# Two short logit blocks in one visit, each merge round in one step, W of two pairs in one, and a new order of the steps

## The chip, the cores and the metric

The kernel runs on one core of one Trainium2 chip. The metric is the device time of one execution in microseconds (us). A core has a tensor engine (PE) with its weight loader (PEld), a vector engine (DVE), a scalar engine (ACT), a general engine (POOL) and a queue engine (SP) that issues transfers (DMAs). The engines run side by side and wait for each other by semaphores.

## The reference, cut to what matters

One decoder layer on 512 tokens of width 1024, all in float32: a norm, one input projection, two groups of eight heads side by side (block-sparse attention with a relative bias, and a gated delta rule in chunks of 64), one output projection, and an MLP of width 4096.

```python
h = rms_norm(x, pre_mix_norm)
att_q, att_k, att_v, gdn_qkv, gdn_z, gdn_a, gdn_b = split(h @ w_in)
# attention: at 512 tokens and blocks of 256 every past block is chosen, so it is causal
logits = q @ k.T * scale + rel_bias[bucket(distance)]
o_att  = softmax(causal(logits)) @ v
# gated delta rule, chunks of 64 tokens
a_mat = eye(64) + strict(k_beta @ k.T * decay)          # unit lower triangular
u, w  = solve(a_mat, v * beta), solve(a_mat, k_beta * exp(g_cum))
def step(state, chunk):                                  # 8 chunks, one after the other
    v_new = u - w @ state
    o     = q_dec @ state + (q @ k.T * decay) @ v_new
    state = state * exp(g_last) + k_dec.T @ v_new
x = x + rms_norm(concat(o_att, norm(o) * silu(z)) @ w_out, post_mix_norm)
h = rms_norm(x, pre_mlp_norm)
x = x + rms_norm(square(relu(h @ w_up)) @ w_down, post_mlp_norm)
```

## The kernel before

The first half of the layer (0 to about 300 us) is woven from generators. `Weave` holds a list of names, `STEPS`; it takes the first name in the list whose generator is ready, and runs that generator to its next `yield`. What PE does is issued in exactly that order. DVE, ACT and POOL are ordered by a scheduler, in which `LEAD` raises the priority of a kind of step; SP is ordered by hand from the loads of the output weights on. The MLP behind it (about 300 to 609 us) is ordered by hand on all engines.

The generators, and the names that they leave in the rows:

- `projections` (rows `ps_mm<-hT_h,w_hi`, `hT_l,w_hi`, `hT_h,w_lo`): the input projection. Weights and activations are split into a high and a low part, so each of the eight steps of an output block is three matmuls. `ORDER` lists the blocks: q, k, v of the delta rule, its gate z, and x, y for the attention; `w0` is V of the attention, made by token (`w_hi,hT_h`) in four banks, one of them in `ps_mm`. One step of `projections` is three matmuls, and they fill the room between all other work. The weights are cast on ACT (L137) and their low part is made on DVE or POOL (L138); `LO_DVE` says which.
- `chunks`: the matrices of a pair of heads for the delta rule (`RC,picks`; `ident,sqt` are transposes of the squares of q; `LWQ,kraw` is k and q against k inside a chunk).
- `scores`: attention logits of a pair of heads, one visit for each block q of 128 queries, with 128(q+1) keys, in the order q = 3, 2, 1, 0 (rows `ps_a<-pt`, six matmuls of 64 rows each); then for each head and block a minimum on DVE (L672) and an exponential on ACT (L674).
- `values`: for each block of keys, transposes of the exponentials (`ident,L`), a copy from the bank by ACT (`ph`, L700), and at last the transposed sums (`ident,R`), and the product with V (`ph,V`), which takes a bank `ps_a`.
- `inverse`: 31 rounds on DVE that invert the 32 x 32 diagonal blocks of `a_mat`. `scan` then merges them to 64 x 64: round 1 (`uap,NT`, 32 x 32 tiles), a copy by ACT, and round 2 (`inv,uap`). It makes W (`inv,kB`, 64 x 64 tiles) and runs the eight chunks (`S,LWQ`, `vn,kdec`, `vn,AT`, `vB,inv`). `z` is one of two halves of the heads; each half is four heads, two pairs.
- `finish_o` norms the output of the scan (`ot`, transposes `ident,ot`, product with the gate `om`, its high part `mg_h`).
- `weights_out` loads the output weights (`wo_raw`, L124), of which two buffers are there for the first eight; ACT casts them (`wo_h`, L125) and DVE makes the low part (L126). `output` is the output projection (`wo_h,mg_h`).
- `normed` norms x of a block of tokens, stores it (`d_x`, L996) and transposes it; `weights_up` and `up0` load the first up-projection's weights (the last ones by L132, `w_raw`) and run it (`mg_h,w_hi`).

Pieces of one kind that follow each other on PE are called a visit. The functions that the diff touches are these:

Of the kernel before, what the change touches and what calls it, by code (L numbers as in the profile page):

```python
# [11 lines left out]
FT = mybir.dt.float32  # L12
# [7 lines left out]
STEPS = "constants_in0 chunks1 constants_in0 bias0*3 chunks0 chunks2 chunks3 scalars0*2 ev0 ev1 ev_q0*2 ev_k0*2 inverse0 scores0 projections0 values0 projections0 scalars0 projections0 scalars0 projections0*5 bias0 projections0 ev2 projections0*4 scores0 ev0 projections0*2 ev1 projections0*2 ev3 scores0 values0 scalars0 chunks2 projections0*2 ev2 chunks0 scores0 chunks1 projections0*2 ev3 projections0 chunks3 chunks0 projections0 scores0 chunks0 projections0 scores0 ev4 chunks1 projections0 ev1 chunks1 projections0 ev3 projections0*4 ev4 projections0 chunks0 chunks1 projections0 chunks0 ev5 projections0 chunks0 projections0*5 chunks1 ev4 projections0 chunks1*2 projections0 ev5 ev6 projections0*8 ev7*2 projections0 chunks2*2 ev6 chunks2 projections0 chunks2 projections0*4 chunks3 projections0 chunks2 projections0 ev8 chunks3*2 projections0*4 chunks3 chunks2*2 projections0*3 ev8 projections0 ev_q1*2 projections0 chunks3 ev8 chunks3 projections0*5 chunks3 inverse0*5 projections0*12 inverse0 projections0*6 inverse0 projections0*2 inverse0 projections0*6 inverse0 projections0*5 inverse0 projections0 inverse0 projections0*2 values0 ev9 projections0*4 inverse0 values0 projections0 inverse0 projections0 inverse0*2 values0 chunks3 projections0 values0 projections0 inverse0*2 ev10 projections0 values0 projections0 inverse0 projections0 values0 projections0*4 inverse0 projections0 ev11 projections0*3 ev9*2 inverse0 projections0*2 ev10*2 inverse0 projections0 inverse0 projections0*7 inverse0 projections0 ev11 inverse0 projections0 inverse0 ev11 inverse0 projections0 ev_k1*2 projections0 ev12 scores0 projections0*3 ev12 projections0 inverse0 ev12 inverse0 projections0*2 inverse0 projections0*2 ev_q2*2 scores0 projections0 inverse0 projections0*2 inverse0*2 weights_out0 weights_up0 scan0 scores0 values0*2 projections0 scores0 projections0*2 values0 scores0 projections0*2 ev_k2*2 projections0 up00 output0 scores0 values0 scan0 scores0 values0*2 scan0 values0 scores0 scan0*3 scores0 projections0 scan0 values0*2 scores0 projections0 scan0 projections0 scores0 values0 scan0 scores0 values0 projections0 scan0*5 projections0*5 scan0 ev_q3*2 projections0*2 scan0 projections0*2 scan0 projections0*2 scan0 finish_o0 projections0 values0 scan0 values0*2 projections0 scan0 projections0 ev_k3 scores0 projections0 ev_k3 scan0 projections0 scan0 scores0 scan0 finish_o0 projections0 finish_o0 finish_o1 projections0*3 ev13 scores0 values0 ev13 values0 scan0 finish_o1*2 projections0*3 scan0 scores0 scan0 projections0 values0 scores0 finish_o2 projections0 scan0 projections0*3 ev14 scan0 ev14 values0 scores0 finish_o0*2 finish_o1 projections0 finish_o2 finish_o1 projections0 finish_o2*3 projections0 scan0 projections0*3 scan0 finish_o3 weights_out0 projections0*2 ev15 finish_o3 ev15 projections0 values0 weights_out0 values0 finish_o3*3 finish_o0 weights_out0*2 finish_o1 weights_out0*9 values0 finish_o2 weights_up0 weights_out0 output0 weights_out0*2 output0 later0 output0*2 weights_out0*2 later0 finish_o3 weights_up0 output0*10 weights_up0 output0*5 later0*2 output0 weights_up0 output0*5 weights_up0 output0 weights_up0 output0*4 weights_up0 output0*2 weights_up0 output0*6 normed0 normed1 output0*6 weights_up0 output0*9 normed2 output0 normed0 output0 weights_up0 output0 normed1 weights_up0 output0*10 up00 output0*2 normed3 up00 normed2 up00*2 normed3 up00*3"  # L20

LEAD = {'chunks': 100, 'inverse': 50, 'scan': 100, 'scores': 100, 'values': 300, 'finish_o': 200, 'take': 50, 'take_a': 100, 'scalars': 50}
# [5 lines left out]
ORDER = "k0 q0 x0 y0 k1 q2 q1 k2 k3 z0 q3 x1 w0 v1 v3 v2 v0 y1 x2 y2 x3 y3 z2 z1 z3"  # L28
LO_DVE = (22, 53)
# [42 lines left out]
def layer(ctx, tc, nc, x, x_t, x_t0, w_first, w_in, w_v, w_ab, w_out, w_up, w_down, conv_w, a_log, dt_bias, gdn_norm_w, rel_bias,  # L72
# [8 lines left out]
    def mm(o, l, r, **kw):  # L81
        nc.tensor.matmul(o, l, r, **kw)  # L82
# [564 lines left out]
    def scores():  # L647
        for p in range(4):
# [12 lines left out]
            for q in (3, 2, 1, 0):  # L661
                w = 128 * q + 128
                qs = slice(128 * q, 128 * q + 128)
                s = [bank("a") for _ in range(2)]
                for n, (i, j) in enumerate(((0, 2), (0, 3), (1, 2))):
                    for hh in range(2):
                        hs = slice(64 * hh, 64 * hh + 64)
                        mm(s[hh][:, :w], T[i][hs, qs], T[j][hs, :w], start=n == 0, stop=n == 2)
                for hh in range(2):
                    l = Ls[hh][:, 64 * q * (q + 1):64 * q * (q + 1) + w]  # L670
                    rows_of[p, hh, q] = l
                    nc.vector.tensor_tensor_reduce(out=l, in0=s[hh][:, :w], in1=Es[hh][:, w - 1::-1], scale=1.0, scalar=3e38,  # L672
                                                   op0=OP.add, op1=OP.min, accum_out=mins[:, q, hh:hh + 1])
                    act(l, l, AF.Exp, bias=mins[:, q, hh:hh + 1], scale=-1.0, accum_out=sums[:, q, hh:hh + 1])  # L674
                yield
                mark(f"row{p}{q}")
# [76 lines left out]
    def scan():  # L753
# [11 lines left out]

        for z in range(2):
            if z:
                yield
            p1 = bank(shape=(128, 4, 4, 32))
            for h in range(4):  # L770
                for t in range(4):
                    for c in range(2):
                        a, b = slice(64 * c, 64 * c + 32), slice(64 * c + 32, 64 * c + 64)
                        mm(p1[b, h, t], NT[a, 4 * z + h, t, 32:64], uap[z][a, h, t], start=True, stop=True,
                           tile_position=(64 * c, 64 * c + 32))
            for c in range(2):
                b = slice(64 * c + 32, 64 * c + 64)
                nc.scalar.copy(uap[z][b], p1[b])
        mark("p1")
        yield  # L780
        for z in range(2):
            if z:
                yield
            p2 = bank(shape=(128, 4, 4, 32))
            for h in range(4):
# [743 lines left out]
```

## Time and profile before

| | |
|---|---|
| time of one execution, median of 3 runs | 616.49 us (615.99 to 616.88) |
| profiled execution: its own time | 617.12 us |
| profiled execution: span of its profile | 615.3 us, mean granted clock 0.997 |
| last input projection ends | 235.4 us |
| output projection starts | 243.1 us |
| merge and scan | 167 to 232 us |
| transfers | 113.21 MB, mean 184 GB/s |

The rows are read so: start or group, length in us, engine, line of the kernel, operation, output<-inputs, and for a matmul rows x columns of the tile in the array, the shape of the moving operand and a count. In brackets stands how long the engine was idle before it, and who released it. "Busy" of PE includes a slow start; the start of the next row tells what a row cost.

### The profile page before, as it was taken

What the parts mean: (1) busy time and instruction counts of PE and PEld (TensorE: products, weight loads), DVE (VectorE), ACT (ScalarE), POOL (GpSimd) and SP (SyncE); (2) the same over time, 40 slices, a digit from 0 to 9 for tenths busy, and PEclk for the clock granted to TensorE, in tenths of its full rate; (3) what the DMA queues carried; (4) which work ended last, traced back from release to release, by engine and by line L of the source; (5) the groups of instructions that cost most, each with busy time, mean ns of one, the idle gap of its engine ahead of it and who ended that gap; (6) DMA issues with size and microseconds to landing.
All of it is one profiled execution on the core that took longest, in us unless ns stands there. A gap on an engine that the chain in (4) does not pass through costs nothing.

```text
span 615.3 us, 11043 instructions
## 1 busy us (share of the span) xinstructions
PE 604.2 (98%) x4281; PEld 516.7 (84%) x4281; DVE 475.5 (77%) x685; ACT 369.0 (60%) x645; POOL 138.0 (22%) x179
## 2 busy tenths in 40 slices
PE   9999999999999998999999999999999999999995
PEld 7777777878778786888999999999998888888884
DVE  6679973899735767757799878787788888887785
ACT  7379773354686686534358565755575557565663
POOL 1556845101231211025022231222121310000000
PEclk9999999999999999999999999999999999999998
DMA  8332324222722124813769998999999999768403
GB/s 310 92 112 85 89 87 100 96 79 85 176 76 79 36 65 138 312 70 136 291 170 317 252 249 233 280 268 211 277 313 327 299 296 285 244 218 301 165 0 137
DMA packets 61156, 113.21 MB, mean 184 GB/s; under 512 B 15784, under 2 KB 35368, under 8 KB 60720
## 3 DMA queue, kind: packets, MB, share of 16 engines
q1 hardware_dynamic: 43120, 82.89, 39.4%
q0 software_dynamic: 17696, 29.36, 22.8%
q8 instruction: 33, 0.54, 0.3%
q10 hardware_dynamic: 288, 0.26, 0.1%
q14 instruction: 19, 0.16, 0.1%
HBM read 106.71 MB, written 35.15 MB: 231 GB/s over the span
## 4 chain that ended last, share of the span: by engine, by line
PE 78%; issue 9%; DMA 5%; DVE 4%; ACT 1%; POOL 1%; SPq 0%; POOLq 0%; ACTq 0%; DVEq 0%
PE ps_mm L82 40%; PE ps_g L82 20%; PE ps_a L82 16%; DMA wo_raw<-in_w_out 2%; PE ps_a L85 2%; DMA xy<-d_x 1%; PE ps_g L85 1%; DMA w_raw<-in_w_up 1%; DVE wo_l L126 1%; POOL rkq L175 1%; DVE xs L995 0%; DMA ww<-in_w_first 0%; DMA w_raw<-in_w_in 0%; DVE conv L365 0%; ACT wo_h L125 0%
## 5 line engine op out<-in xcount | busy, mean ns | idle before, releaser
L113 ACT CAST wdh<-wd 128x1024 fp32r<-128x1024 f32 x53 | 55.9, 1054 | 51.4 <-PE ps_mm L82 22.6
L113 ACT CAST u_h<-w 128x1024 fp32r<-128x1024 f32 x49 | 51.0, 1045 | 51.2 <-DVE w L1139 15.6
L114 DVE TENSOR_TENSOR wdl<-wd,wdh 128x1024 fp32r<-128x1024 f32 x53 | 64.9, 1224 | 21.5 <-ACT wdh L113 21.4
L114 DVE TENSOR_TENSOR u_l<-w,u_h 128x1024 fp32r<-128x1024 f32 x49 | 59.9, 1224 | 23.4 <-ACT u_h L113 23.3
L82 PE MATMUL ps_mm<-hT_h,w_hi 128*128 128x512 f32 x168 | 71.0, 423 | 0.3 <-DVE w_hi L241 0.3
L82 PE MATMUL ps_mm<-hT_l,w_hi 128*128 128x512 f32 x168 | 65.9, 392 | 0.0
L82 PE MATMUL ps_mm<-hT_h,w_lo 128*128 128x512 f32 x168 | 65.9, 392 | 0.0
L1172 POOL DMA_DIRECT2D d_T<-in_w_down x32 | 33.0, 1032 | 142.2 <-DMA d_T<-in_w_down 77.5
L137 ACT CAST w_hi<-w_raw 128x512 fp32r<-128x512 f32 x50 | 31.0, 620 | 41.1 <-PE ps_g L82 9.7
L82 PE MATMUL ps_mm<-wdh,u_h 128*128 128x512 f32 x116 | 45.2, 390 | 0.0
L82 PE MATMUL ps_mm<-wdl,u_h 128*128 128x512 f32 x116 | 45.1, 389 | 0.0
L82 PE MATMUL ps_mm<-wdh,u_l 128*128 128x512 f32 x116 | 45.1, 389 | 0.0
L82 PEld LDWEIGHTS ps_mm<-hT_h,w_hi 128*128 128x128 f32 x168 | 31.7, 189 | 10.7 <-issue 3.8
L82 PEld LDWEIGHTS ps_mm<-hT_h,w_lo 128*128 128x128 f32 x168 | 31.5, 188 | 7.0
L82 PEld LDWEIGHTS ps_mm<-hT_l,w_hi 128*128 128x128 f32 x168 | 31.8, 190 | 4.9
L114 DVE TENSOR_TENSOR u_l<-f,u_h 128x1024 fp32r<-128x1024 f32 x28 | 34.1, 1219 | 0.0
L138 POOL TENSOR_TENSOR w_lo<-w_raw,w_hi 128x512 fp32r<-128x512 f32 x22 | 28.5, 1297 | 23.0 <-ACT w_hi L137 20.6
L82 PE MATMUL ps_g<-wdh,u_h 128*128 128x512 f32 x80 | 31.1, 389 | 0.0
L82 PE MATMUL ps_g<-wdl,u_h 128*128 128x512 f32 x80 | 31.1, 389 | 0.0
L82 PE MATMUL ps_g<-wdh,u_l 128*128 128x512 f32 x80 | 31.1, 389 | 0.0
L113 ACT CAST u_h<-f 128x1024 fp32r<-128x1024 f32 x28 | 29.3, 1045 | 0.0
L138 DVE TENSOR_TENSOR w_lo<-w_raw,w_hi 128x512 fp32r<-128x512 f32 x28 | 22.1, 790 | 5.0 <-ACT w_hi L137 4.9
(484 smaller groups left out, 1829.5 us busy)
## 6 DMA issues: line engine op xcount, KB each, us to landing
d_T<-in_w_down POOLq DMA_DIRECT2D x48, 512.0 KB, 10.7
wd<-d_T SPq DMA_DIRECT2D x32, 512.0 KB, 6.2
w<-in_w_up SPq DMA_DIRECT2D x28, 512.0 KB, 7.3
wd<-in_w_down SPq DMA_DIRECT2D x24, 512.0 KB, 7.2
w_raw<-in_w_in SPq DMA_DIRECT2D x40, 256.0 KB, 2.6
wo_raw<-in_w_out SPq DMA_DIRECT2D x16, 256.0 KB, 3.2
d_T<-d_T POOLq DMA_DIRECT2D x8, 512.0 KB, 11.5
ww<-in_w_first SPq DMA_DIRECT2D x8, 256.0 KB, 5.6
```

Of the source, the lines that this page charges most:

```text
L82: nc.tensor.matmul(o, l, r, **kw)
L85: nc.tensor.transpose(o, i, ident[:k, :k])
L113: nc.scalar.copy(hi, src)
L114: tt(lo, src, f32(hi), op=OP.subtract)
L126: (sub or tt)(lo, raw, f32(hi), op=OP.subtract)
L137: nc.scalar.copy(hi, raw)
L138: (sub or tt)(lo, raw, f32(hi), op=OP.subtract)
L175: nc.gpsimd.tensor_tensor(r, r, m, op=OP.pow)
L1172: nc.gpsimd.dma_start(d_T[t][k], block(b, second)[k], accum_op=OP.add, max_dma_last_dim=1024)
```

## The change

It does four things.

1. `scores`: the blocks q=1 and q=0 share a pair of banks and one visit: first both blocks' matmuls, then their minima and exponentials. Three visits for each of four pairs in place of four.
2. `scan`, merge: round 1 of both halves is one step, with the copies behind it, and so is round 2. The `yield` between the halves goes.
3. `scan`, W: `kB` of both pairs of a half are made first, in a tag of four buffers instead of a single buffer of its own, and the matmuls of both follow in one visit: two visits in place of four.
4. `STEPS` is another list, `LEAD` has other priorities, `ORDER` other places for v, x2, y2 and z3, and `LO_DVE` moves one low part from DVE to POOL.

PE keeps its 3758 instructions, ACT its 597 and SP its 239; DVE goes from 687 to 686, POOL from 184 to 185.

```diff
-STEPS = "constants_in0 chunks1 constants_in0 bias0*3 chunks0 ...
-LEAD = {'chunks': 100, 'inverse': 50, 'scan': 100, 'scores': 100, 'values': 300, 'finish_o': 200, 'take': 50, 'take_a': 100, 'scalars': 50}
+STEPS = "chunks1 constants_in0*2 chunks3 bias0*2 scalars0 ...
+LEAD = {'chunks': 25, 'inverse': 0, 'scan': 50, 'scores': 400, 'values': 300, 'finish_o': 400, 'take': 50, 'take_a': 300, 'scalars': 0}
-ORDER = "k0 q0 x0 y0 k1 q2 q1 k2 k3 z0 q3 x1 w0 v1 v3 v2 v0 y1 x2 y2 x3 y3 z2 z1 z3"
-LO_DVE = (22, 53)
+ORDER = "k0 q0 x0 y0 k1 q2 q1 k2 k3 z0 q3 x1 w0 v3 v0 v1 v2 y1 y2 x2 x3 y3 z2 z3 z1"
+LO_DVE = (23, 51)
...
-            for q in (3, 2, 1, 0):
-                w = 128 * q + 128
-                qs = slice(128 * q, 128 * q + 128)
+            for group in ((3,), (2,), (1, 0)):
                 s = [bank("a") for _ in range(2)]
-                for n, (i, j) in enumerate(((0, 2), (0, 3), (1, 2))):
+                of_q = {q: slice(256 * i, 256 * i + 128 * q + 128) for i, q in enumerate(group)}
+                for q, o in of_q.items():
+                    qs, ks = slice(128 * q, 128 * q + 128), slice(0, 128 * q + 128)
+                    for n, (i, j) in enumerate(((0, 2), (0, 3), (1, 2))):
+                        for hh in range(2):
+                            hs = slice(64 * hh, 64 * hh + 64)
+                            mm(s[hh][:, o], T[i][hs, qs], T[j][hs, ks], start=n == 0, stop=n == 2)
+                for q, o in of_q.items():
+                    w = 128 * q + 128
                     for hh in range(2):
...
                 yield
-                mark(f"row{p}{q}")
+                for q in group:
+                    mark(f"row{p}{q}")
...
+        both = []
         for z in range(2):
-            if z:
-                yield
             p1 = bank(shape=(128, 4, 4, 32))
+            both.append(p1)
...
+        for z, p1 in enumerate(both):
             for c in range(2):
                 b = slice(64 * c + 32, 64 * c + 64)
                 nc.scalar.copy(uap[z][b], p1[b])
-        mark("p1")
         yield
...
         for z in range(2):
             wps = [bank(shape=(128, 2, 4, 64)) for _ in range(2)]
+            kBs = []
             for p in (2 * z, 2 * z + 1):
-                kB = sc.tile([128, 512], FT, name="kB", bufs=1).rearrange("p (t h e) -> p t h e", t=4, h=2)
+                kB = sc.tile([128, 512], FT, name="kB", tag="ot", bufs=4).rearrange("p (t h e) -> p t h e", t=4, h=2)
...
-                yield
+                kBs.append((p, kB))
+            yield
+            for p, kB in kBs:
                 for t in range(4):
```

Round 2 is changed as round 1 is. Three places show how the new order stands against the old one.

**PE at the merge.** `ident,L` are transposes of pair 1's exponentials, `uap,NT` is round 1, `inv,uap` round 2, `pt` logits, `ph,V` the product with V. Before:

```order
L85 MATMUL ps_a<-ident,L 128x128 x6
L82 MATMUL ps_g<-uap,NT 32x32 x32
L85 MATMUL ps_a<-ident,L 128x128 x8
L85 MATMUL ps_a<-ident,R_1950 128x128 x4
L82 MATMUL ps_g<-uap,NT 32x32 x32
L82 MATMUL ps_a<-ph,V 64x128 x2
L82 MATMUL ps_a<-ph,V 64x256 x2
L82 MATMUL ps_a<-ph,V 64x384 x2
L82 MATMUL ps_a<-ph,V 64x512 x2
L82 MATMUL ps_a<-pt 128x512 x6
L82 MATMUL ps_g<-inv,uap 32x32 x64
```

After:

```order
L85 MATMUL ps_a<-ident,L 128x128 x6
L82 MATMUL ps_g<-uap,NT 32x32 x64
L85 MATMUL ps_a<-ident,L 128x128 x8
L85 MATMUL ps_a<-ident,R_1946 128x128 x4
L82 MATMUL ps_g<-inv,uap 32x32 x64
L82 MATMUL ps_a<-pt 128x512 x6
L82 MATMUL ps_a<-ph,V 64x128 x2
L82 MATMUL ps_a<-ph,V 64x256 x2
```

Both halves of round 1 are one run, and between it and round 2 stand twelve transposes; the product with V and the logits of 512 keys have moved behind round 2.

**ACT at the end of the scan.** The exponentials (`L,sums<-L,mins`) are those of the last pair's blocks q=1 (256 keys) and q=0 (128). Before:

```order
L674 ACTIVATE L,sums<-L,mins 128x256 x2
L847 COPY vn<-ps_g 64x256 x2
L137 CAST w_hi<-w_raw 128x512
L700 COPY ph<-ps_a 128x512
L674 ACTIVATE L,sums<-L,mins 128x128 x2
L679 COPY R_2903<-sums 128x512
L869 COPY ot<-ps_g 64x2x128 x2
L125 CAST wo_h<-wo_raw 128x512 x2
L847 COPY vn<-ps_g 64x256 x2
```

After:

```order
L125 CAST wo_h<-wo_raw 128x512 x2
L855 COPY vn<-ps_g 64x256 x2
L435 ACTIVATE t_2850<-zs 128x512
L125 CAST wo_h<-wo_raw 128x512 x2
L677 ACTIVATE L,sums<-L,mins 128x256
L677 ACTIVATE L,sums<-L,mins 128x128
L704 COPY ph<-ps_a 128x512
L677 ACTIVATE L,sums<-L,mins 128x256
L677 ACTIVATE L,sums<-L,mins 128x128
```

The four exponentials stood ahead of the casts of output weights 1 and 2, and stand now behind the casts 1 to 4 (counted from 0).

**SP at the first up-projection.** `w_raw` are its last weights, `d_x` a store of normed x, `xs` a load of x. Before:

```order
L132 DMA w_raw<-in_w_up 128x2x256
L996 DMA d_x<-xs 128x1024
L946 DMA xs<-in_x 128x1024
L132 DMA w_raw<-in_w_up 128x2x256
L996 DMA d_x<-xs 128x1024
```

After:

```order
L132 DMA w_raw<-in_w_up 128x2x256
L1004 DMA d_x<-xs 128x1024
L132 DMA w_raw<-in_w_up 128x2x256
L1004 DMA d_x<-xs 128x1024
L954 DMA xs<-in_x 128x1024
```

The second load of weights has moved ahead of one store and one load of x. One place more is told in words: of pair 3's chunk matrices the `LWQ,kraw` visit stood behind V's first 15 matmuls and stands now ahead of V, between the transposes `ident,sqt` and V.

More of the change, by code (lines that the diff above doesn't have):

```diff
@@ L660, in scores @@
             sums = at.tile([128, 4, 2], FT, name="sums")
-            for q in (3, 2, 1, 0):
-                w = 128 * q + 128
-                qs = slice(128 * q, 128 * q + 128)
+            for group in ((3,), (2,), (1, 0)):
                 s = [bank("a") for _ in range(2)]
-                for n, (i, j) in enumerate(((0, 2), (0, 3), (1, 2))):
-                    for hh in range(2):
[L667 to L674, printed above, removed]
+                of_q = {q: slice(256 * i, 256 * i + 128 * q + 128) for i, q in enumerate(group)}
[7 more added lines that the diff above has]
+                    w = 128 * q + 128
+                    for hh in range(2):
+                        l = Ls[hh][:, 64 * q * (q + 1):64 * q * (q + 1) + w]
+                        rows_of[p, hh, q] = l
+                        nc.vector.tensor_tensor_reduce(out=l, in0=s[hh][:, o], in1=Es[hh][:, w - 1::-1], scale=1.0, scalar=3e38,
+                                                       op0=OP.add, op1=OP.min, accum_out=mins[:, q, hh:hh + 1])
+                        act(l, l, AF.Exp, bias=mins[:, q, hh:hh + 1], scale=-1.0, accum_out=sums[:, q, hh:hh + 1])
                 yield
-                mark(f"row{p}{q}")
+                for q in group:
+                    mark(f"row{p}{q}")
             nc.vector.reciprocal(sums, sums)
@@ L778, in scan @@
                 nc.scalar.copy(uap[z][b], p1[b])
-        mark("p1")
         yield
+        both = []
         for z in range(2):
-            if z:
-                yield
             p2 = bank(shape=(128, 4, 4, 32))
+            both.append(p2)
             for h in range(4):
@@ L790, in scan @@
                            tile_position=(64 * c + 32, 64 * c))
+        for z, p2 in enumerate(both):
             for c in range(2):
@@ L802, in scan @@
                 nc.gpsimd.tensor_tensor(kd, kd, b2(egd), op=OP.mult)
-                yield
+                kBs.append((p, kB))
+            yield
+            for p, kB in kBs:
                 for t in range(4):
```

2 lines of the change are left out of this document (1 added, 1 removed).

## The prediction

> **What bounds the kernel now.** I read the page's busy time first, then its chain, then the waits of the tensor engine (PE), then windows by stage, and last the timeline of PE around every visit that the change touches.
>
> ```profile
> PE 604.2 (98%) x4281; PEld 516.7 (84%) x4281; DVE 475.5 (77%) x685; ACT 369.0 (60%) x645; POOL 138.0 (22%) x179
> ...
> PE 78%; issue 9%; DMA 5%; DVE 4%; ACT 1%; POOL 1%; SPq 0%; POOLq 0%; ACTq 0%; DVEq 0%
> ...
> 165.00:243.00 78.00, 76.39 (x1118) 59.16 (x1116) 46.82 (x108) 57.48 (x138) 15.38 (x22) 1.00 0.27 77
> ...
> 300.00:547.00 247.00, 247.00 (x1702) 231.04 (x1701) 210.14 (x200) 150.60 (x184) 45.98 (x57) 1.00 0.98 270
> ```
>
> PE is busy 98% of the span and holds 78% of the chain. The two window rows give start and end, length, then busy time of PE, weight load, DVE, ACT and POOL. From 165 to 243 us, where the merge and the scan stand, PE has 1.6 us free. From 300 to 547 us (the MLP) it has none. So time is won only where PE spends its slots badly (a slow start after another kind of matmul counts as busy) or where it waits:
>
> ```profile
> PE ps_a L82 <- ACT ph L700: 1.3, 1, 1.3
> ...
> PE ps_mm L82 <- DVE pt L626: 0.5, 1, 0.5
> PE ps_mm L82 <- ACT mg_h L113: 0.3, 1, 0.3
> ...
> PE ps_mm L82 <- ACT w_hi L137: 0.3, 1, 0.3
> PE ps_mm L82 <- DVE w_lo L138: 0.2, 1, 0.2
> PE ps_g L85 <- DVE kraw L370: 0.2, 1, 0.2
> ```
>
> Columns: total, times, longest. Every wait is a single event; the six make 2.8 us.
>
> **Part 1: what a change of kind costs on PE.** Here is a stretch of W and of logits, by start and length. PE issues in order, so start to next start is what a piece costs.
>
> ```profile
> 167.44 1.20 PE L82 MATMUL ps_g<-uap,NT 32*32 32x32 f32 x64
> 168.57 1.09 PE L85 MATMUL ps_a<-ident,L 128*128 128x128 f32 x8
> ...
> 176.51 0.79 PE L82 MATMUL ps_a<-pt 64*128 64x384 f32 x6
> 177.22 0.50 PE L82 MATMUL ps_mm<-hT_h,w_hi 128*128 128x512 f32 x1
> ...
> 179.11 0.62 PE L82 MATMUL ps_a<-pt 64*128 64x256 f32 x6
> 179.66 0.50 PE L82 MATMUL ps_mm<-hT_h,w_hi 128*128 128x512 f32 x1
> ...
> 181.18 0.50 PE L82 MATMUL ps_mm<-hT_h,w_hi 128*128 128x512 f32 x1
> 181.52 0.39 PE L82 MATMUL ps_mm<-hT_l,w_hi 128*128 128x512 f32 x1
> 181.75 0.40 PE L82 MATMUL ps_mm<-hT_h,w_lo 128*128 128x512 f32 x1
> 182.08 0.55 PE L82 MATMUL ps_a<-pt 64*128 64x128 f32 x6
> 182.56 0.66 PE L85 MATMUL ps_a<-ident,L 128*128 128x128 f32 x4
> 183.14 0.69 PE L82 MATMUL ps_g<-inv,kB 64*64 64x64 f32 x32
> 183.77 0.87 PE L85 MATMUL ps_a<-ident,L 128*128 128x128 f32 x6
> 184.40 0.48 PE L82 MATMUL ps_mm<-hT_h,w_hi 128*128 128x512 f32 x1
> 184.71 0.39 PE L82 MATMUL ps_mm<-hT_l,w_hi 128*128 128x512 f32 x1
> ```
>
> A projection matmul costs 0.23 (181.52 to 181.75). The first after a visit costs 0.34 (181.18 to 181.52), after transposes 0.31 (184.40); the last ahead of logits costs 0.33 (181.75 to 182.08). A visit thus charges the projections on its two sides about 0.21 beyond its own slot.
>
> *Logits.* The visit of 128 keys costs 0.48 (182.08 to 182.56), that of 256 keys 0.55 (179.11 to 179.66), that of 384 keys 0.71 (176.51 to 177.22). The six matmuls of q=0 and the six of q=1 stream 384 columns each pair, as much as the 384 visit; with twelve starts in place of six I take 0.71 to 0.85. Instead of 1.03 that saves 0.18 to 0.32, and with 0.21 at the sides 0.39 to 0.53; over four pairs 1.6 to 2.1. Where the removed visit stood between transposes, less goes at the sides: low end 1.3.
>
> *W.* Two visits of four go. A visit of 32 costs 0.63 (183.14 to 183.77); the columns that stream are the same in a visit of 64, so the 0.21 at the sides goes and perhaps 0.1 of its own entry and exit. Twice that: 0.6, bounds 0.2 and 0.7. The two kB are now made ahead on POOL into a four-buffer tag, ahead of the visit; POOL has 15.4 of 78 us busy there, so I charge nothing; without that cover one of them would stand in front of PE.
>
> *Round 1.* One visit of 64 costs 1.13 (167.44 to 168.57). Two halves in one run save one entry and exit: 0.2, bounds 0 and 0.4. Round 2 ran as one piece already.
>
> *Against it.* Counting pieces in the two orders, runs of projections rise from 56 to 59, since three times more something now stands inside them: minus 0.2 each at most, 0.3 to 0.6. Sum of part 1: 1.7 + 0.6 + 0.2 - 0.4 = 2.1 saved; bounds 1.1 and 3.1. I take 2.2.
>
> The Trainium skill, TensorEngine Tiling (Array Packing), Key Properties, says that changing the tiling mode drains the engine and changing the tile does not. By that rule only changes of tile size count, 72 ahead of the output projection before and 59 after; at about 0.11 each it gives an estimate of 1.4 saved in place of 2.2, and 614.0 in all. The trace agrees for 64 rows but not for transposes, whose tile is that of the projections and after which the first still costs 0.31.
>
> **Part 2: stalls that the new order removes, keeps or makes.**
>
> ```profile
> 93.39 0.60 PE L85 MATMUL ps_g<-ident,sqt 128*128 128x128 f32 x4
> 94.47 0.50 PE L82 MATMUL ps_mm<-w_hi,hT_h 128*128 128x512 f32 x1 [0.48 <-DVE pt L626]
> ...
> 87.95 0.32 PE L82 MATMUL ps_g<-LWQ,kraw 64*64 64x128 f32 x1
> ...
> 88.99 0.50 PE L82 MATMUL ps_mm<-hT_h,w_hi 128*128 128x512 f32 x1
> ...
> 286.95 0.75 SPq L132 DMA_DIRECT2D w_raw<-in_w_up  x1
> ...
> 291.31 0.28 PE L82 MATMUL ps_mm<-mg_h,w_lo 128*128 128x256 f32 x1
> 291.86 0.39 PE L82 MATMUL ps_mm<-mg_h,w_hi 128*128 128x256 f32 x1 [0.28 <-ACT w_hi L137]
> ...
> 292.59 0.39 PE L82 MATMUL ps_mm<-mg_h,w_lo 128*128 128x256 f32 x1 [0.22 <-DVE w_lo L138]
> ```
>
> *Start of V.* Four transposes should cost 0.4 (six cost 0.63); PE needed 1.08 from 93.39 to 94.47, so 0.65 is lost waiting for the `ps_mm` bank of x1. In the new order one more chunk visit (1.04, 87.95 to 88.99) stands between x1 and V. That covers it, if its own inputs are there; I take 0.35 saved, bounds 0 and 0.65. *kraw:* its transposes move back by about a dozen projections; 0.2 saved, bounds 0 and 0.2.
>
> *Last weights of the first up-projection.* They were issued on SP at 286.95, behind a store of `d_x` that had to wait; PE then lost 0.43 at 291.31 (0.55 in place of 0.12) and as much again until 292.59. In the new order that load stands one store and one load of x earlier. Saved 0.8, bounds 0.4 and 0.8.
>
> *End of the layer's first half.* Block (1, 0) of the last pair now comes later, and its four exponentials stand on ACT behind two more casts of output weights:
>
> ```profile
> 236.29 0.62 ACT L125 CAST wo_h<-wo_raw 128x512 fp32r<-128x512 f32 x1 [0.97 <-DMA wo_raw<-in_w_out]
> 237.84 0.62 ACT L125 CAST wo_h<-wo_raw 128x512 fp32r<-128x512 f32 x1 [0.93 <-DMA wo_raw<-in_w_out]
> 238.48 1.07 ACT L700 COPY ph<-ps_a 128x512 f32<-128x512 f32 x2
> ...
> 239.12 2.37 PE L82 MATMUL ps_a<-ph,V 128*64 128x128 f32 x16 [1.34 <-ACT ph L700]
> 241.42 1.32 PE L85 MATMUL ps_g<-ident,ot 128*128 128x128 f32 x8
> 243.09 0.50 PE L82 MATMUL ps_mm<-wo_h,mg_h 128*128 128x512 f32 x1 [0.34 <-ACT mg_h L113]
> ...
> DMA to landing us min/median/max: 2.5/3.2/5.7
> ```
>
> Before, the product with V waited 1.3 because the copy at 238.48 stood behind a cast whose weights had not landed. With what follows (1.67 from 241.42 to 243.09 for eight transposes worth 0.9) the end loses 2.1 us. In the new order the copy that frees the product's bank still stands behind such casts. Followed step by step with these durations (casts 0.62, exponentials of 0.4 to 0.5, copies 0.5, landings after 3.2), I find about 0.5 at the transposes of block 1, 0.3 at block 0, 0.4 at the start and 0.4 in the product, 0.4 at the first cast of `om`: 2.0. So 0.1 saved; bounds 1.0 saved and 3 lost.
>
> *New waits.* Round 2 of the merge must not start before ACT has copied both halves (four copies of 0.6); twelve transposes stand between, about 1.5 us, and the second half's copies are wanted 1 us later still. I charge 0.4 for this and other unseen waits; bounds 0 and 1.5.
>
> **Sum.** 2.2 + 0.35 + 0.2 + 0.8 + 0.1 - 0.4 = 3.25 saved. The profiled execution took 617.12 (span 615.3, 1.8 around it) and becomes 613.9; it lies 0.6 above the median of 616.49, so the median becomes 613.2. The MLP behind it has the same instructions and order and follows PE, so it moves as a whole.
>
> **Rivals.** (a) *The exponentials behind the casts.* Each cast is tied to its load, and two buffers make each load wait for the cast two before. If two loads in a row take the longest landing, 5.7, in place of 3.2, the end loses 5 more than 2.0 and all else is given back: 618.2, slower. It decides from 3.3 more on; with 4.5 more it is slower by over 0.2%. For it: the 0.97 and 0.93 that ACT waited for weights. Against: 3.2 is the median, and only two such landings in a row do it.
>
> The Trainium skill, PSUM, Engine vs sequencer instructions, calls the queues of ScalarE and VectorE strictly first in, first out, which is this rival's ground; the copy at 238.48, right behind a cast that waited 0.93, agrees.
>
> (b) *Changes of kind are only moved.* More runs of projections, and the side costs come back elsewhere: part 1 gives nothing, stalls 1.45 less 1.0 for new waits: 616.0, no change. The 0.31 after transposes speaks for it; that sixteen visits of logits really become twelve speaks against. The same time results if transfers pace the MLP (0.98 of the time some transfer runs) and keep its end in place; against that, PE has no gap in that window.
>
> (c) *Nearly all stalls go.* Part 1 at 3.1, stalls 2.8, no new ones: 610.6.
>
> **Chances.** My forecast, 611.6 to 615.0 about 613.2: 0.66. Rival (a): 0.10 slower or, milder, 0.03 level. (b): 0.10. (c): 0.11. Below 0.2% (1.2 us) this kernel's runs cannot be told from no change; so faster than 615.3: 0.77, same 0.14, slower 0.09. The range that leaves 2 in 10 out takes in (b) and most of (c): 610.8 to 616.1.
>
> **What would show it.** Right: the 128-key visits are gone and one of 0.7 to 0.85 stands per pair; `ps_mm <- pt` and the two waits on w_hi and w_lo vanish from PE's waits; the output projection starts near 240 and the MLP 3 us earlier. Wrong: a wait on ps_a for ph or L of 3 us or more near 232 to 240, a wait of round 2 for `uap`, or an output start as early as forecast with an end that does not move.

## The result, and the profile after

| | before | after |
|---|---|---|
| median of four runs each, same chip | 616.29 us (615.99 to 616.88) | 613.39 us (612.29 to 613.77) |
| ratio, with its 95% interval | | 0.9949 [0.9932, 0.9966] |
| profiled execution | 617.12 us, span 615.3 | 613.05 us, span 611.3 |

The change is 2.9 us faster, with 613.2 forecast. Run again later beside the kernel before, it gave the same ratio, 0.9949 [0.9936, 0.9962], from four executions of 612.84 to 614.81; a fifth took 1524, with PE busy for 1515 of them, and is left out.

First the page of after: busy time, then the chain's shares by engine, and below them the window of merge and scan (start and end, length, then PE, weight load, DVE, ACT, POOL).

```profile
PE 601.4 (98%) x4281; PEld 516.4 (84%) x4281; DVE 477.5 (78%) x684; ACT 367.4 (60%) x645; POOL 141.4 (23%) x180
...
PE 77%; issue 10%; DVE 6%; DMA 4%; ACT 2%; SPq 1%; POOLq 0%; DVEq 0%
```

```profile
165.00:243.00 78.00, 76.69 (x1120) 60.11 (x1119) 47.99 (x107) 56.28 (x137) 14.41 (x20) 1.00 0.24 73
```

PE still bounds the kernel with the same 4281 instructions (the page counts what ran; the 3758 given with the change stands in no page) and is busy 2.8 us less; the span is 4.0 shorter. The window's busy share hardly tells anything: the same 78 us now hold work that used to end later. The waits of PE tell more (total, times, longest):

```profile
PE ps_a L85 <- ACT L L677: 1.3, 2, 0.8
PE ps_a L82 <- DVE rs L188: 1.1, 1, 1.1
PE ps_mm L82 <- DVE conv L365: 1.0, 1, 1.0
PE ps_mm L82 <- DVE w_hi L241: 0.3, 1, 0.3
```

The two lines on `rs` and on L241 belong to the start of the kernel and stood there before. All six waits that the prediction quoted are gone from the list: `ph`, `pt`, `mg_h`, `w_hi` of L137, `w_lo`, `kraw`. Two others took their place, on L (the exponentials) and on `conv`, 2.3 us together. Now the timeline of PE at the visits that were merged (start, length):

```profile
160.91 0.48 PE L82 MATMUL ps_mm<-hT_h,w_hi 128*128 128x512 f32 x1
161.23 0.40 PE L82 MATMUL ps_mm<-hT_l,w_hi 128*128 128x512 f32 x1
161.46 0.40 PE L82 MATMUL ps_mm<-hT_h,w_lo 128*128 128x512 f32 x1
161.79 0.91 PE L82 MATMUL ps_a<-pt 64*128 64x256 f32 x12
162.63 0.50 PE L82 MATMUL ps_mm<-hT_h,w_hi 128*128 128x512 f32 x1
...
179.86 1.16 PE L82 MATMUL ps_g<-inv,kB 64*64 64x64 f32 x64
180.95 0.91 PE L82 MATMUL ps_a<-pt 64*128 64x256 f32 x12
181.78 0.50 PE L82 MATMUL ps_mm<-hT_h,w_hi 128*128 128x512 f32 x1
```

The row at 160.91 follows two transposes. A visit of twelve costs 0.84 (161.79 to 162.63) where the two of six cost 1.03. A W visit of 64 costs 1.09 (179.86 to 180.95) where two of 32 cost 1.26, and here the logits stand right behind it, with no projection between. Next the three places where PE now loses time, first PE, then who was late:

```profile
143.02 0.40 PE L82 MATMUL ps_mm<-hT_h,w_lo 128*128 128x512 f32 x1
144.44 0.47 PE L82 MATMUL ps_mm<-hT_h,w_hi 128*128 128x512 f32 x1 [1.02 <-DVE conv L365]
...
231.25 0.55 PE L85 MATMUL ps_a<-ident,L 128*128 128x128 f32 x3 [0.44 <-ACT L L677]
232.61 0.55 PE L85 MATMUL ps_a<-ident,L 128*128 128x128 f32 x3 [0.81 <-ACT L L677]
...
240.97 0.48 PE L82 MATMUL ps_mm<-wo_h,mg_h 128*128 128x512 f32 x1
```

```profile
140.61 1.11 DVE L751 COPY inv<-inv 128x1024 f32<-128x1024 f32 x1
...
143.54 0.76 DVE L365 SCALAR_TENSOR_TENSOR conv<-ps_mm,cw,conv 128x509 f32<-128x509 f32 x1
```

```profile
230.07 0.62 ACT L125 CAST wo_h<-wo_raw 128x512 fp32r<-128x512 f32 x1 [0.96 <-DMA wo_raw<-in_w_out]
230.60 0.50 ACT L677 ACTIVATE L<-L,mins 128x256 f32<-128x256 f32 x1
...
231.95 0.51 ACT L677 ACTIVATE L<-L,mins 128x256 f32<-128x256 f32 x1
```

The row at 240.97 is the start of the output projection. At 143 us the closing copy of the inverse (L751, 1.1 us) stands on DVE in front of the convolution that frees a projection's bank. At 231 us the exponentials of the last pair's block stand on ACT behind a cast that waited 0.96 for its weights: this is what rival (a) was about, at a price of 1.6.

The last matmul of the profiled execution starts 3.5 us earlier (the span is 4.0 shorter, since what stands behind that matmul is 0.6 shorter too). Where the 3.5 lie, by the start of a row before and after:

| place | before | after | moved |
|---|---|---|---|
| 25th projection matmul | 11.32 | 11.03 | -0.29 |
| round 1 starts (`uap,NT`) | 167.44 | 166.69 | -0.75 |
| last projection matmul | 235.20 | 234.84 | -0.36 |
| output projection starts | 243.09 | 240.97 | -2.12 |
| first up-projection starts | 288.92 | 286.43 | -2.49 |
| MLP starts (`ma_h,u_h`) | 314.70 | 311.18 | -3.52 |
| last matmul | 608.27 | 604.77 | -3.50 |

The first row is not the work of the change. PE issues the same matmuls up to there in both kernels, but the first ones stand 0.41 to 0.56 apart in place of 0.23, five of them before and three after. Here are two of the slow ones and the 25th, before, and the 25th after:

```profile
6.16 0.63 PE L82 MATMUL ps_a<-hT_h,w_hi 128*128 128x512 f32 x1
6.58 0.57 PE L82 MATMUL ps_mm<-hT_l,w_hi 128*128 128x512 f32 x1
...
11.32 0.39 PE L82 MATMUL ps_mm<-hT_h,w_hi 128*128 128x512 f32 x1
```

```profile
11.03 0.39 PE L82 MATMUL ps_mm<-hT_h,w_hi 128*128 128x512 f32 x1
```

In the kept profiles of all variants (the execution of 1524 us aside) the 25th starts anywhere from 10.28 to 11.49, so 0.3 of every later row is scatter, and 3.2 at the last matmul are left for the change.

The MLP itself takes 293.6 in both. Ahead of the output projection I add up what PE lost beyond the usual distance of two rows. Before: 0.6 at kraw, 0.65 at V, 1.34 at the product and 0.77 at the transposes behind it, 3.4 in all. After: 0.2 at 114.8, 1.2 at `conv`, 1.6 at L and 0.4 in the product, 3.4 in all. The lost time there is equal, so of the 2.1 saved there 0.3 are the start and I put the other 1.8 down to changes of kind. The remaining 1.4 lie behind the start of the output projection: 0.4 in it and 1.0 in the first up-projection, which now takes 24.75 in place of 25.79.

### The profile page after: what moved, and what is told of

The parts are those of the page before. It is cut to its first block, busy times and chain, and to the rows that moved or that the text cites. A ratio compares the mean times of both kernels' runs of the same rounds, so it can differ in the third digit from the quotient of the medians.

```text
span 611.3 us, 11049 instructions
## 1 busy us (share of the span) xinstructions
PE 601.4 (98%) x4281; PEld 516.4 (84%) x4281; DVE 477.5 (78%) x684; ACT 367.4 (60%) x645; POOL 141.4 (23%) x180
## 4 chain that ended last, share of the span: by engine, by line
PE 77%; issue 10%; DVE 6%; DMA 4%; ACT 2%; SPq 1%; POOLq 0%; DVEq 0%
PE ps_mm L82 38%; PE ps_g L82 21%; PE ps_a L82 15%; DVE inv L748 2%; DVE pr L747 2%; PE ps_a L85 2%; PE ps_g L85 1%; DMA wo_raw<-in_w_out 1%; DMA xy<-d_x 1%; DVE conv L365 1%; DVE w_lo L138 1%; DMA inv<-d_n 1%; DMA d_n<-NT 1%; DMA ww<-in_w_first 0%; ACT wo_h L125 0%
## 5 line engine op out<-in xcount | busy, mean ns | idle before, releaser
L137 ACT CAST w_hi<-w_raw 128x512 fp32r<-128x512 f32 x50 | 31.1, 621 | 45.3 <-DMA w_raw<-in_w_in 10.0
## 6 DMA issues: line engine op xcount, KB each, us to landing
d_T<-d_T POOLq DMA_DIRECT2D x8, 512.0 KB, 10.6
```

Of the source, the lines that this page charges most:

```text
L137: nc.scalar.copy(hi, raw)
```

## The experiments

The times of all are medians of four to eleven executions, with the kernel before run beside them on the same chip (616.8 to 617.06). They are compared by their ratios to it, and stages by the rows of the profiled execution.

**The merged logits alone, in the old order.**

```diff
-            for q in (3, 2, 1, 0):
+            for group in ((3,), (2,), (1, 0)):     # before, with part 1 of the change
...
-... values0*2 scores0 projections0 scan0 projections0 scores0 values0 ...
+... values0*2 scores0 projections0 scan0 projections0 values0 ...          # q=0's own step goes, four times
```

> The kernel before with part 1 alone: blocks q=1 and q=0 in one visit, at the place where q=1 stood, all else in the old order. Theory (a change of kind costs PE slots): each merged visit takes about 0.83 in place of 0.55 + 0.48 and the projections beside it lose one slow start, 0.3 a pair, so the output projection starts about 1.2 us earlier (243.1 to about 241.9) and the time falls by 0.9 to 1.4, to about 615.2. Rival (the new order brings the gain, the merged visits only move their cost): no change, 616.0 to 616.6, output projection at 243.0 or later because the wait for ph at its end is tied to the loads of output weights and takes up what was saved.

Measured: 622.05 us, ratio 1.0083 [1.007, 1.0097], 5.2 slower. Its waits of PE:

```profile
PE ps_mm L82 <- ACT mg_h L113: 1.7, 1, 1.7
...
PE ps_g L85 <- ACT sqt L405: 1.2, 1, 1.2
...
PE ps_g L82 <- ACT LWQ L815: 1.0, 1, 1.0
PE ps_g L82 <- DVE S L869: 0.9, 1, 0.9
```

The four merged visits with those of q=3 and q=2 take 9.8 us of PE, before 10.6. The new waits, with the slow starts behind them, come to 6.3, and the last matmul is 5.2 later: the merge itself saves PE about 1.1, not the 1.7 that I took. Four exponentials that come at once on ACT make other work late: from 54.39 they stand there in front of `sqt`, which starts at 56.16 and for which PE waits 1.2, and from 181.13 in front of `LWQ` (183.78). So in the old order the merge costs more than it saves.

**The merge and W alone, in the old order.**

```diff
+        both = []                                  # before, with parts 2 and 3 of the change
...
-... scores0 values0*2 scan0 values0 scores0 scan0*3 ...
+... scores0 values0*2 values0 scores0 scan0*3 ...                           # a step of scan goes, four times
```

> The kernel before with parts 2 and 3 alone (rounds of the merge in one step, W of two pairs in one visit), old order. Theory: W 0.3 of its own and about 0.3 beside it, round 1 0.1 and 0.2 beside it, so 0.6 to 0.9 earlier after W and the time about 615.6. Rival (the wait at the end of the scan is set by the output weights' loads, which do not move): PE 0.7 earlier at the first step of the scan, and nothing of it left at the output projection, 616.3.

Measured: 617.02 us, ratio 1.0001 [0.9992, 1.001], no change. In the trace the last matmul is 0.85 earlier, which is the size I gave (0.6 and 0.2), but 0.86 of it is there already when V starts, 75 us ahead of the merge (91.86 before, 91.00 here), where both kernels take the same steps, and it arises in the slow matmuls at the start (the 25th projection matmul stands at 10.30 here). So this is scatter. What parts 2 and 3 save on PE goes to waits: the wait for `ph` is 1.5 in place of 1.3, that for `mg_h` 0.6 in place of 0.3, for `w_hi` 0.6 in place of 0.3.

**The changed kernel with q=1 and q=0 in two visits again.**

```diff
-            for group in ((3,), (2,), (1, 0)):
+            for q in (3, 2, 1, 0):                 # after, with part 1 undone
...
-... projections0 scores0 projections0 values0 ...
+... projections0 scores0 projections0 scores0 projections0 values0 ...     # one projection step between, four times
```

> The changed kernel with part 1 alone undone: q=1 and q=0 in two visits, q=0 one projection step behind. Theory: 0.3 a pair lost, 1.2 in all, time about 614.6 against 613.4, and the extra stands in the logits' slots and the projections beside them. Rival (order brings the gain): no more than 0.3 lost, 613.4 to 613.7. The last pair's block q=0 is asked one projection later, so the wait for the exponentials at block 1 of its transposes (1.6 us in the changed kernel) may also shrink, which would hide 0.3 of the loss.

Measured: 619.67 us, ratio 1.0041 [1.0027, 1.0054], by the ratios 5.7 more than the changed kernel, and slower than before. Two rows of its waits, and the windows at the start of its output projection (the eighth column is the granted clock):

```profile
PE ps_mm L82 <- ACT mg_h L113: 1.5, 1, 1.5
PE ps_a L82 <- DVE mins L672: 1.4, 2, 0.9
```

```profile
244.00:247.00 3.00, 1.40 (x7) 0.73 (x6) 2.50 (x5) 2.18 (x4) 0.00 (x0) 1.00 0.87 257
247.00:251.00 4.00, 4.00 (x12) 3.14 (x12) 3.78 (x7) 2.75 (x5) 0.00 (x0) 0.58 1.03 322
```

It takes 1.8 more up to the last chunk of the scan (225.92 for its last `S,LWQ`, after 224.08), or 2.4 counted from the 25th projection matmul. Of this 0.5 is the first of the new waits for `mins`; the rest is near the 1.6 to 2.1 that four visits should cost by the prediction. The other 5.1 are lost between there and the first up-projection, in waits that also let the clock fall to 0.58; seven matmuls then stand 0.43 apart in place of 0.23, 1.4 us. So undoing part 1 costs far more than the visits, because the order was chosen for it.

**The last up-projection weights loaded later.**

```diff
-... output0*2 normed1 output0*2 weights_up0 output0*9 normed2 normed0 ...
+... output0*2 normed1 output0*2 output0*9 normed2 weights_up0 normed0 ...   # after; this load behind one more store of x
```

> The changed kernel with one load moved: the last weights of the first up-projection are issued on SP behind the store of the third block of x again, as they were before. Theory: the load goes out some 7 us later (near 283.3 in place of 276.2), lands near 287.5 to 288, and PE loses 0.4 to 0.8 before it reaches the MLP; time 613.9 to 614.2. Rival (the load has room even there, the gain at that place came from the earlier start of all): no change, 613.4, and no wait on w_hi or w_lo in PE's waits.

Measured: 614.11 us, ratio 0.9957 [0.9944, 0.997]. Where the load stands on SP, what PE then waits for, and ACT between them:

```profile
282.83 0.43 SPq L132 DMA_DIRECT2D w_raw<-in_w_up  x1
```

```profile
290.35 0.39 PE L82 MATMUL ps_mm<-ma_h,wu 128*128 128x256 f32 x1 [0.48 <-DVE xs L1002]
```

```profile
286.64 0.62 ACT L137 CAST w_hi<-w_raw 128x512 fp32r<-128x512 f32 x1 [2.97 <-DMA w_raw<-in_w_up]
287.16 0.59 ACT L997 ACTIVATE xs<-ps_mm 128x512 f32<-128x512 f32 x1
```

In the changed kernel the load is issued at 276.16, here 6.7 later, behind a store. The first up-projection takes 25.51 in place of 24.75: 0.76 of the 0.8 that I predicted comes back. The wait has another name, though, xs and not the weights: on ACT the cast that waits for the late weights stands in front of the squares (L997) that the norm of x needs, and PE waits for the bank that this norm frees.

**All eight first casts of output weights on POOL.**

```diff
     def load_split(hi, lo, src, sub=None, raw=None, cast=None):
...
-        nc.scalar.copy(hi, raw)
+        (cast or nc.scalar.copy)(hi, raw)
...
-                               raw=wpool.tile(...))
+                               raw=wpool.tile(...), cast=nc.gpsimd.tensor_copy if b == 0 else None)
```

> The changed kernel with the casts of the first eight blocks of output weights on POOL in place of ACT; PE's order is the same. Theory (ACT's exponentials and copies stand behind casts that wait for their loads): the two waits for L at block 1's transposes (1.6 us of PE) and most of the 0.4 at the last product vanish; POOL's casts are slower than ACT's 0.62, so the last of the eight lands up to 3 us later, which the output projection may feel at its fourth to eighth block of weights. Output projection starts at 239.0 to 239.6 in place of 241.0, time 611.4 to 612.4. Rival (the exponentials are late by themselves, behind DVE's minima or the logits): waits for L of 1 us or more stay and the time does not change.

Measured: 616.44 us, ratio 0.9993 [0.9983, 1.0003]. The new wait of PE, POOL's row behind it, and the window after it:

```profile
PE ps_g L85 <- DVE ot L895: 3.2, 1, 3.2
```

```profile
236.79 1.64 POOL L175 TENSOR_TENSOR oss<-oss,mhalf 128x8 f32<-128x8 f32 x1
238.42 0.95 POOL L125 CAST wo_h<-wo_raw 128x512 fp32r<-128x512 f32 x1
```

```profile
242.00:246.00 4.00, 3.60 (x11) 2.94 (x12) 2.62 (x5) 1.10 (x4) 0.00 (x0) 0.60 0.69 209
```

The waits for L are gone, so the casts were their cause. But the casts now wait for their weights on POOL, in front of the norm of the last `ot` (`oss`), and PE stood still for 3.2 us and went on at 0.60 of its clock. The casts themselves were not slow: five of the eight took 0.61 or 0.62, as on ACT, and the longest 1.16. Nor is POOL all of it. The last step of `oss` ends there at 239.53, and DVE begins the `ot` that needs it only at 241.66, behind three other operations (`t`, `mg_l` and a `wo_l`); in the changed kernel it begins at 239.35.

```profile
241.66 0.68 DVE L895 TENSOR_TENSOR ot<-ot,oss 128x512 f32<-128x512 f32 x1
```

**The inverse's closing copy on ACT.**

```diff
-        nc.vector.tensor_copy(iT, iU.rearrange("p j i -> p i j"))
+        nc.scalar.copy(iT, iU.rearrange("p j i -> p i j"))
```

> The changed kernel with the closing copy of the inverse (1024 elements a partition, 1.11 us on DVE, between two pieces of v's convolution) on ACT. Theory (v's convolution holds the ps_mm bank because the copy and the rounds stand in DVE's queue ahead of its pieces): PE's wait for conv falls from 1.0 to 0.0 to 0.3 and the time by 0.8 to 1.1, to about 612.5. Rival (the merge or the scan, not this bank, is late behind it): the wait goes and comes back at the first merge round or at uap, time 613.4.

Measured: 613.52 us, ratio 0.9953 [0.994, 0.9965]. The wait for `conv` is gone, which fits the copy as its cause. The scheduler also moved a low part of weights (0.7) from ahead of that piece of `conv` to behind it, so the copy is not shown to be the whole of it. Another wait on DVE came, and the time is the changed kernel's within what can be measured:

```profile
PE ps_a L82 <- DVE mins L675: 0.8, 1, 0.8
```

The last matmul is 0.33 earlier (604.44). **Both last edits together:**

> Both of these. If the two waits are independent, the gains add up: 610.4 to 611.6. If the end of the scan is set by the loads of the output weights, which are asked when buffers come free and not when PE gets there, the gain of the earlier one is eaten at the end and the time is that of the casts on POOL alone.

Measured: 615.45 us, ratio 0.9977 [0.9968, 0.9987], with a wait of 3.1 for `ot` and one of 1.6 for `mins`. Neither wait that the edits removed was a gain, alone or together; the time is near that of the casts on POOL, as the second theory has it.

**Pair 3's chunk visit back behind V's first fifteen matmuls.**

```diff
-... ev8 chunks3*2 inverse0*3 projections0 inverse0 projections0*3 inverse0*2 ...
+... ev8 chunks3 projections0*5 chunks3 inverse0*6 ...                      # after; as the order before had it
```

> The changed kernel with pair 3's within-chunk visit back behind V's first 15 matmuls. Theory (the prediction's): the wait for the ps_mm bank of x1 at V's start returns, 0.65 to 0.75 of PE, time 614.0. Rival: the wait at V's start returns, but the wait for conv at 143 us (1.0) shrinks by as much, since that one is set by DVE's chain and not by PE: time 613.4.

Measured: 612.8 us, ratio 0.995 [0.993, 0.9969], the same as the changed kernel. The wait of 0.5 for `pt` at V's start is back and the wait for `conv` is gone. Having that visit ahead of V thus bought the start of V and paid for it 50 us later, where the inverse's last rounds meet the convolution. The edit puts six steps of the inverse back with the visit, so it does not tell which of the two moves those rounds.

**Three runs on the end of the first half.** The first is the changed kernel unaltered, beside the others.

> The changed kernel unaltered, beside the next two, so that they can be compared with it on one chip. Expected by every theory: 613.4, ratio to the kernel before 0.995.

Measured: ratio 0.9949 [0.9936, 0.9962], as given with the result. The stages of the changed kernel are still read from its first profile.

```diff
-... cast=nc.gpsimd.tensor_copy if b == 0 else None)
+... cast=nc.gpsimd.tensor_copy if b == 0 and (z or not k) else None)        # weights 0 to 4 on POOL, 5 to 7 on ACT
```

> The changed kernel with the casts of output weights 0 to 4 on POOL and only 5 to 7 still on ACT. Theory (the two waits of the transposes for L, 1.6 us in all, come from exponentials that stand on ACT behind casts whose weights have not landed, and the price of moving all eight casts was POOL's late work for the last norm of ot): the exponentials now stand ahead of all casts on ACT, POOL is done with its casts about 2 us before the norm's sums are there; the waits for L go, no wait for ot as long as 1 us takes their place, the output projection starts about 1.5 us earlier (239.5 in place of 241.0), the time is about 611.9, ratio 0.993. Rival (the slack behind the last matmuls of the scan is the product's and the norm's, and any gain at L is lost to them): the waits for L go, waits for ot, mins or mg_h of the same sum appear, and the time stays 613.0 to 614.0. Third (the clock falls again after a stretch with little on PE): 615 or more, with matmuls 0.4 apart at the start of the output projection.

Measured: 613.08 us, ratio 0.9944 [0.9928, 0.9961]. PE at the output projection, and below it DVE and ACT:

```profile
238.65 0.66 PE L85 MATMUL ps_g<-ident,ot 128*128 128x128 f32 x4 [0.83 <-DVE om L904]
...
240.73 0.50 PE L82 MATMUL ps_mm<-wo_h,mg_l 128*128 128x512 f32 x1 [0.61 <-DVE mg_l L114]
```

```profile
237.24 0.69 DVE L126 TENSOR_TENSOR wo_l<-wo_raw,wo_h 128x512 fp32r<-128x512 f32 x1 [0.94 <-ACT wo_h L125]
237.85 0.74 DVE L904 SCALAR_TENSOR_TENSOR om<-ps_g,nw,zs 128x512 f32<-128x512 f32 x1
```

```profile
236.59 0.62 ACT L125 CAST wo_h<-wo_raw 128x512 fp32r<-128x512 f32 x1 [1.01 <-DMA wo_raw<-in_w_out]
```

The waits for L are gone, none for `ot` came, the output projection starts 1.6 earlier, of which 0.7 were there before the scan; and yet from the last `S,LWQ` to the first up-projection it takes 62.32, where the changed kernel takes 62.35. All of it came back as waits for `om` and `mg_l`: DVE makes the low part of a weight in front of `om`, and that waits for a cast whose weights landed late. So the rival was right, with other names for the waits. With the visit of pair 3 put back as well, as shown above:

> As the last, and pair 3's visit inside the chunks back behind the first fifteen matmuls of V, where the order before had it. Theory (moving that visit ahead of V bought the start of V, 0.7, and paid with the wait for the cast of the inverse, 1.0, so putting it back is worth 0.3 to 1.0; the two edits lie 90 us apart and add): last matmul 1.5 + 0.6 earlier than in the changed kernel, time about 611.3, ratio 0.992, below both kernels. Rival (the gain of putting it back, not separable in its own run, 612.8 in the range 612.3 to 615.9, was scatter): the same time as the run with the casts alone, within 0.3.

Measured: 613.65 us, ratio 0.9939 [0.9926, 0.9953]. The same stage takes 62.00; its waits are again `om` (0.6) and `mg_l` (0.5). The medians of these two cannot be told from the changed kernel's. They hide something, though: by their granted clocks, the two executions of the last run at 0.998 and 0.999 took 611.98 and 611.69, near the 611.3 of the theory, and the three at 0.994 and 0.995 took 613.92 to 614.31.

**The low parts of weights 6 and 7 on POOL as well.** Now no low part that waits for a load stands on DVE in front of `om`.

```diff
-... cast=nc.gpsimd.tensor_copy if b == 0 and (z or not k) else None)        # the last kernel
+... cast=nc.gpsimd.tensor_copy if b == 0 and (z or not k) else None, sub=nc.gpsimd.tensor_tensor if b == 0 and not z and k > 1 else None)
```

> As the last, and the low parts of output weights 6 and 7 on POOL in place of DVE. In the two last runs the waits for L were gone, but om on DVE stood behind a low part whose cast waited 1.0 for its weights, and PE waited 0.6 to 0.8 for om and 0.5 to 0.6 for mg_l, so the output projection began only 1.3 to 1.6 earlier and ended no earlier than the stages ahead of it explain. Theory (what holds the end of the half is only where the work that depends on these loads stands in the queues of ACT and DVE): now om and the first mg_h stand ahead of the low parts and casts that wait; the waits for om and mg_l go, the output projection starts 0.9 and ends 1.4 earlier than in the last run, and the profiled run takes 610.2 to 610.6. Rival (the loads of the output weights themselves pace this stage, two buffers and about 3 us to land): a wait for wo_h or wo_l of the same 1.4 takes the place inside the output projection, its end stays, and the profiled run takes 611.4 to 612.

Measured: 611.53 us (611.26 to 612.61), ratio 0.9916 [0.9903, 0.993]. DVE and ACT at the place, and what is left of PE's wait:

```profile
236.85 0.75 DVE L904 SCALAR_TENSOR_TENSOR om<-ps_g,nw,zs 128x512 f32<-128x512 f32 x1
```

```profile
237.63 0.62 ACT L113 CAST mg_h<-om 128x512 fp32r<-128x512 f32 x1 [0.59 <-DVE om L904]
```

```profile
PE ps_g L85 <- DVE om L904: 0.3, 1, 0.3
```

The stage takes 61.27, 0.73 less than in the last run and 1.1 less than in the changed kernel, and no wait for `wo_h` or `wo_l` took its place: the loads do not pace this stage, their place in the queues does. It is half of the 1.4 that I expected: no load stands directly in front of `om` any more, but the `zs` ahead of it waits 1.47 for ACT's `t`, which stands behind a cast that still waited 0.64 for its weights, and PE still waits 0.3 for `om`. The profiled execution took 611.26, between the two forecasts, since it also came 0.6 later to the scan (`S,LWQ` starts at 190.40, in the last run at 189.78), where the steps are the same. This kernel's interval lies below that of the changed one: it is faster than both, than the changed one by 0.3%. Its median is 2.1 below that of the last run, more than the 0.73 of the stage; all its executions had a clock of 0.997 or more, so a part of the 2.1 may be the clock and not the edit.

One thing limits all small readings here. Six of the variants (the late load, the casts on POOL, the copy on ACT, both, weights 0 to 4 on POOL, and the changed kernel itself) take the same steps up to the start of V, and it starts there between 89.85 and 90.83. That scatter is made in the slow matmuls at the kernel's start: counted from the 25th projection matmul, V starts 79.31 to 79.38 later in all six. The absolute start of a row thus says nothing of a difference under 1 us; starts counted from there, waits and lengths of stages are steadier.

## Why the prediction was right

The sum held: 3.25 saved forecast, 3.2 at the last matmul when the scatter of the start is set off, 2.9 between the medians. That it is so close is luck, since errors of opposite sign cancel: 0.4 too much for changes of kind and 1.0 too little for new waits, against 0.3 too little at V, 0.4 at kraw, 0.2 at the last up-weights and 0.4 in the output projection, which I had not forecast. By its steps:

- *Changes of kind, 2.2.* What is left ahead of the output projection, with equal waits and without the start, is 1.8. (My sum of this part gives 2.1, and its terms give bounds of 0.9 and 2.9; the 2.2, the 1.1 and the 3.1 have no reason beside them.) The parts are less sure. The twelve-matmul visit cost 0.84, inside my 0.71 to 0.85, and runs of projections rose from 55 to 59 (I had counted 56 to 59). But the logits alone gave 1.1, where I took 1.7 and gave 1.3 as the low end. This term was mis-sized. The rest of the 1.8 may come from the new order, which puts visits of different kinds side by side, as at 180.95; no run separates it.
- *Rule by tile size, 1.4 in place of 2.2.* The 1.8 lies halfway and decides nothing. But the first projection after two transposes still costs 0.32 (160.91 to 161.23 in after), with no change of tile. The rule in the Trainium skill, TensorEngine Tiling (Array Packing), Key Properties, does not foresee this.
- *Start of V, 0.35, and new waits, 0.4.* Both mis-sized. V's start was covered in full, 0.65. The new wait was not in round 2, where there is none, but at `conv`, 1.2, and 0.2 at a low part of weights. The two belong together, as the run with the visit and the steps of the inverse put back shows: it takes the one and gives the other. I had looked for the price of the moved visit only among its own inputs, not at the work on DVE that it lets the inverse overtake.
- *kraw, 0.2.* Gone, worth 0.6 with the slow starts.
- *Last up-weights, 0.8.* Confirmed: 1.0 in the stage, 0.76 back when the load is moved later.
- *End of the first half, 2.0 left of 2.1.* Exactly 2.0 is left, but 1.6 at block 1, where I had 0.5, nothing at block 0 or at `om`, and 0.4 in the product. The sum was right and the places wrong, which is luck too. The last runs show why the sum is the steadier of the two: the waits for L covered a wait at `om` behind the same loads, and PE loses the time in the one place or the other.
- *Rival (a)* needed 3.3 more at that end. Its mechanism is real, since a cast's wait of 0.96 became PE's, but none of the casts behind it waited longer than 0.46 until the output projection started, so the loads landed in time for the rest of that end. In the kernel with split visits two casts waited 1.9 and 1.6, and there 5.1 were lost at that end, 619.67.
- *Rival (b)*, that merging and the new order save nothing, is refuted by the 1.8 that the waits do not explain; its other half, that transfers pace the MLP, by the MLP's constant 293.6. *Rival (c)* lacked the two new waits.

What stays open: how much of the 1.8 belongs to each part, since each part alone, in an order not made for it, brings more waits than it saves.

## What to carry to other kernels

In a kernel that one engine's queue bounds, a merged visit is worth its saved changes of kind only together with an order that spreads the burst it sends to the other engines; the same merge without it cost 5.2 us. When a wait goes, ask which later wait it covered: three edits here removed one and found it again, and the one that paid moved the last steps that depend directly on a late load out from in front of the work that the bounding engine needs. Price a moved step by the work that it now lets pass on the other queues, not only by its own inputs.

## What the hardware showed that I had not expected

A short pause can cost more than its length, and where it falls decides. After 3.2 us without a matmul (eight casts on POOL), PE ran at 0.60 of its clock in the next four us, and after a stretch with 1.40 us of work in 3.0 (split visits) at 0.58; each time seven or so matmuls were 0.43 apart in place of 0.23, some 1.4 us. Yet with the copy on ACT added to the casts on POOL, PE stood still for 3.1 us at the same place and the clock stayed, while a wait of 1.6 us for `mins` earlier in that execution halved it. Its windows (the third column is PE's busy time, the eighth the granted clock):

```profile
156.33:159.74 3.41, 1.79 (x10) 1.05 (x9) 2.39 (x6) 0.94 (x2) 0.00 (x0) 1.00 0.29 99
159.75:163.16 3.41, 3.41 (x12) 2.40 (x9) 1.29 (x6) 2.40 (x8) 0.00 (x0) 0.50 0.24 77
238.26:241.67 3.41, 1.86 (x12) 0.55 (x8) 3.11 (x6) 1.53 (x4) 1.57 (x3) 1.00 0.36 129
241.67:245.08 3.41, 1.90 (x11) 1.63 (x12) 3.32 (x6) 0.93 (x2) 0.00 (x0) 1.00 0.42 121
```

In these traces the granted clock changes only at steps of 3.41 us, whose first lies 4.0 to 7.3 us after the first instruction, at another time in each execution. The wait for `mins` fell into one step, and the pause of 3.1 was cut in two by the border at 241.67. Over the kept profiles, up to the last matmul, each step with at most 1.81 us of PE's work was followed by one at half clock, and none with 1.86 or more was. The Trainium skill, TensorE: Matmul & The Clock Gate, Part 1, says that the clock is halved after an idle window of about 3.4 us, which runs free of the kernel. The traces agree on the length and on the free start, but such a step need not be idle: PE was busy for half of it. The slow matmuls at the start of the kernel end at the first such step, so their number differs from execution to execution. In the changed kernel no later step holds less than 2.39 us of work, and the clock stays at 1.00.
